# Values as the stationary operand in the dilated and the memory attention of a two-layer encoder

## The chip, the cores and the metric

The kernel runs on one core of a Trainium2 chip. The metric is the device time of one execution in microseconds (us). Engines are named as the profile names them: PE is TensorE's matmuls and PEld its weight loads, DVE is VectorE, ACT is ScalarE, POOL is GpSimd, SP is SyncE, whose queue issues the DMAs.

## What is computed

Two sequences of 256 tokens (512 rows in all) of width 1024 go through two layers. Layer 0 mixes with differential attention, layer 1 with dilated attention; each layer also attends with 4 heads of width 64 to 256 memory tokens, and ends with a gated ConvFFN. The parts that the change touches are the last steps of the two attentions:

```python
def memory_attention(xq, mk, mv):                 # both layers, 4 heads of 64
    s = einsum('bqhd,bkhd->bhqk', xq, mk) / sqrt(64)
    pr = softmax(s, axis=-1)
    return einsum('bhqk,bkhd->bqhd', pr, mv)

def dilated_mixer(...):                           # layer 1, 8 heads of 64, 3 groups of keys
    # per group: banded scores over residue classes, lse, pr = exp(s - lse), o = pr @ v
    w = softmax(stack(lses), axis=0)              # over the groups
    o = einsum('gbsh,gbshd->bshd', w, stack(outs))
```

The three groups of the dilated mixer, weighted by the softmax of their log-sums, are one softmax over all their keys together, and the kernel computes it so: for a tile of 128 queries and one head, the scores against 256 keys of group 0, 128 of group 1 and 128 of group 2 stand side by side in one 128x512 tile, with a mask.

## The kernel before

All activations of 512 tokens are four token tiles (NT = 4) of 128 rows; tiles 0 and 1 are one sequence, 2 and 3 the other. The large products (input projections, output projections, the ConvFFN) are split into a high and a low part: `mm3` (L368 to L370) issues three matmuls (high by high, low by high or high by low) for each 128 rows of contraction. Weights come by DMA (`w_loader`, L334), are split by ACT (L345) and DVE (L347), and wait in six pairs of buffers `wh` and `wl`.

The order of the work is made by a small planner that runs while the kernel is written (`Sched`): each part of the kernel is a generator that yields events or times; every `S.op(engine, cost)` advances that engine by a cost written beside the instruction, and the generator that is due next writes its instructions next. Each engine then runs its instructions in the order in which they were written, and waits where data are missing. So a changed cost or wait in one generator moves the instructions of all others around it. On PE the attention's small matmuls stand between `mm3` groups of the projections of the next pair of heads, or of the output projection at the end of the mixer.

The attention works on pairs of heads. For a token tile `t`, `scores` (L819) writes one 128x512 tile `sc` for each head of the pair; the heads lie on partitions 0 to 63 and 64 to 127 of the queries and keys, and their matmuls alternate. Then, for each head by itself (`unit`): DVE takes the minimum (L800 for memory, L1000 with the mask for dilated), ACT the exponential with its sum (L807, L1006), DVE the reciprocal of the sum into `rs` (L842, L1008), `transpose_e` (L742) turns the four 128x128 blocks of `e` on PE into a bank `tp` and ACT copies them to `eT` (L746), and four fp32 matmuls (L851 for memory, L1019 for dilated) with a block of `eT` as the stationary operand and 64 columns of the values moving add up 64 columns of the bank `o`, queries on partitions. An fp32 matmul shows as two records, one for each pass.

When all units are done, DVE multiplies the bank `o` by `rs` into `on` (L861, L1042), `out_T` (L774) transposes `on` on PE to features on partitions (with the permutation `perm_bwd` in layer 1), and `evac_seq` (L762 on ACT, L764 on DVE) splits the result into the high and low tiles that `out_proj` reads. Buffers: three `e`, three `eT`, two banks each of `sc` and `tp`, one bank `o`. The memory attention (`attn_cross`) runs once in each layer with 8 tiles-by-pairs, the dilated attention (`attn_b`) for four pairs of heads with 4 token tiles each. The differential attention (`attn_a`, L922) keeps its way through `transpose_e` and `out_T`.

Of the kernel before, what the change touches and what calls it, by code (L numbers as in the profile page):

```python
# [149 lines left out]
def c_dve(n, ptr=0, fast=False):  # L150
    return 0.15 + n / 960 + 0.06 * ptr
# [6 lines left out]
def c_mm(n, fp32=False):  # L158
    return n / 2400 * (4 if fp32 else 1) + 0.0135
# [99 lines left out]
def trunk_kernel(ctx: ExitStack, tc: tile.TileContext, io: dict, out: bass.AP):  # L259
# [31 lines left out]
    def sm(n, name):  # L291
        return small.tile([128, n], F32, tag=f"{name}{n}", name=name)
# [296 lines left out]
    def half(h):  # L589
        return slice(64 * h, 64 * h + 64)  # L590
# [177 lines left out]
    def out_T(o, cols, tiles, s, permuted):  # L768

        tp = yield from tp_s.get()  # L770
        for j in range(len(tiles)):
            for i in range(2):
                c = cols[j][i]
                nc.tensor.transpose(tp.v[:, (2 * j + i) * 128:(2 * j + i) * 128 + 128], o.v[:, c:c + 128],  # L774
                                    perm_bwd if permuted else ident)
                te = S.op("PE", T_PE)
        yield te
        for j, (hi, lo) in enumerate(tiles):
            yield from evac_seq(tp.v[:, 256 * j:256 * j + 256], hi, lo, s, permuted)
        tp.done(S.now)  # L780
# [4 lines left out]
        return hi, lo  # L785

    sc_lock = Lock(S)

    def sc_pair():
        yield from sc_lock.get()  # L790
# [37 lines left out]
    def attn_cross(xq_ev, mk_ev, mv_ev, permuted, res):  # L828
        yield xq_ev
        yield mk_ev  # L830
        yield mv_ev
        xqT, mkT, mv = xq_ev.val, mk_ev.val, mv_ev.val
        tiles = []
        for b in range(2):
            x = yield from hi_lo()
            tiles.append(x)
        parts = []

        def unit(t, h, sc, te, o_ev, rs, fin):
# [5 lines left out]
            yield o_ev  # L845
            o = o_ev.val.v.rearrange("p (t b h d) -> p t b h d", t=2, b=2, h=2)
            for b in range(2):
                for kt in range(2):
                    c = kt * 256 + (2 * b + h) * 64
                    i = 2 * b + kt  # L850
                    nc.tensor.matmul(o[:, t % 2, b, h, :], eT.v[:, i * 128:i * 128 + 128], mv[t // 2].v[:, c:c + 64],  # L851
                                     start=(kt == 0), stop=(kt == 1))
                    te = S.op("PE", c_mm(128, True))
            eT.done(te)
            fin.set(te)

        def finish(s, o_ev, rs, fins, part):
            for f in fins:
                yield f
            on = yield from on_s.get()  # L860
            nc.vector.tensor_tensor(on.v.rearrange("p (a d) -> p a d", d=64),  # L861
                                    o_ev.val.v.rearrange("p (a d) -> p a d", d=64),
                                    rs.rearrange("p t b h -> p (t b h)").unsqueeze(2).to_broadcast([128, 8, 64]),
                                    ALU.mult)
            te = S.op("DVE", c_dve(512))
            o_ev.val.done(te)
            yield te
            yield from out_T(on, [[0, 256], [128, 384]], tiles, s, permuted)
            on.done(S.now)
            part.set(S.now)  # L870

        for s in range(2):
            o_ev = S.event()
            rs = sm(8, "rs").rearrange("p (t b h) -> p t b h", t=2, b=2)
            fins = []
            for t in (2 * s, 2 * s + 1):
                sc = yield from sc_pair()
                te = scores(sc, [(256 * b, xqT[b], slice(t * 128, t * 128 + 128), mkT[b],
                                  slice(s * 256, s * 256 + 256)) for b in range(2)])
                for h in range(2):  # L880
                    f = S.event()
                    fins.append(f)
                    S.spawn(unit(t, h, sc[h], te, o_ev, rs, f))
                if t % 2 == 0:
                    S.spawn(take(o_s, o_ev))
            part = S.event()
            parts.append(part)
            S.spawn(finish(s, o_ev, rs, fins, part))
# [98 lines left out]
    def attn_b(q01, q2k0, k12, v01_ev, v2_ev, vcol, last_v2, res):  # L987
        for x in (q01, q2k0, k12):
            yield x
        q = [q01.val[0], q01.val[1], q2k0.val[0]]  # L990
        k = [q2k0.val[1], k12.val[0], k12.val[1]]
        o_ev = S.event()
        rs = sm(8, "rs").rearrange("p (t h) -> p t h", h=2)

        def unit(t, h, sc, te, fin):
            s, qi = divmod(t, 2)
            yield te
            e = yield from e_s.get()
            mn = sm(1, "mn")
            nc.vector.tensor_tensor_reduce(out=e.v, in0=sc.v, in1=mask[:, qi, :], scale=1.0, scalar=BIG,  # L1000
                                           op0=ALU.add, op1=ALU.min, accum_out=mn)
# [9 lines left out]
            yield o_ev  # L1011
            yield v01_ev
            yield v2_ev
            v = [(v01_ev.val, 0), (v01_ev.val, 128), (v2_ev.val, vcol)]
            o = o_ev.val.v.rearrange("p (t h d) -> p t h d", t=NT, h=2)
            for i, (g, kt) in enumerate(((0, 0), (0, 1), (1, qi), (2, qi))):
                vt, c = v[g]
                c += kt * 256 + 64 * h
                nc.tensor.matmul(o[:, t, h, :], eT.v[:, i * 128:i * 128 + 128], vt[s].v[:, c:c + 64],  # L1019
                                 start=(i == 0), stop=(i == 3))  # L1020
                te = S.op("PE", c_mm(128, True))
            eT.done(te)
            fin.set(te)

        fins = []
        for t in range(NT):
            tq = slice(t * 128, t * 128 + 128)
            ks = slice(t // 2 * 256, t // 2 * 256 + 256)
            sc = yield from sc_pair()
            te = scores(sc, [(0, q[0], tq, k[0], ks), (256, q[1], tq, k[1], tq), (384, q[2], tq, k[2], tq)])  # L1030
            for h in range(2):
                f = S.event()
                fins.append(f)
                S.spawn(unit(t, h, sc[h], te, f))
            if t == 0:
                S.spawn(take(o_s, o_ev))
        for f in fins:
            yield f
        for x in q + k + v01_ev.val + (v2_ev.val if last_v2 else []):
            x.done(S.now)  # L1040
        on = yield from on_s.get()
        nc.vector.tensor_tensor(on.v.rearrange("p (a d) -> p a d", d=64),  # L1042
                                o_ev.val.v.rearrange("p (a d) -> p a d", d=64),
                                rs.rearrange("p t h -> p (t h)").unsqueeze(2).to_broadcast([128, 8, 64]),
                                ALU.mult)
        te = S.op("DVE", c_dve(512))
        o_ev.val.done(te)
        yield te
        tile_ = yield from hi_lo()
        for s in range(2):  # L1050
            yield from out_T(on, [[256 * s, 256 * s + 128]], [tile_], s, True)
        on.done(S.now)
        res.set(S.now, tile_)


# [479 lines left out]
```

## Time and profile before

| what | value |
|---|---|
| median of 3 runs | 1406.17 us (1405.69 to 1406.70) |
| the profiled execution's own time | 1404.72 us |
| its span | 1402.9 us |
| PE busy | 1385.6 us, 99% of the span |
| DVE / ACT / POOL busy | 55% / 44% / 20% |

The span runs from the first to the last instruction of the profiled execution. Busy time counts each moment at which at least one instruction of the engine runs. A PE row's duration holds the time until its last result is written, so the rows of neighbouring matmuls overlap; what a matmul takes of PE's time is read from the start of one row to the start of the next. A row of the timeline may merge several instructions of one line (x8, x16); then its start is that of the first.

### The profile page before, as it was taken

Reading aid. Unit: us, or ns where it says so; the run is one execution under the profiler, and the core shown is the slowest. Engines: PE = TensorE matmul, PEld = TensorE weight load, DVE = VectorE, ACT = ScalarE, POOL = GpSimd, SP = SyncE. Lnnn points to the kernel's source line nnn. Section 1 sums busy time; section 2 is a strip of 40 time slices with the busy share of each in tenths; the row PEclk is TensorE's granted clock in tenths of the full one; section 3 lists DMA queues with packets and bytes.
Section 4 is the critical chain, followed back from the end, with each engine's and each line's share of the span. In section 5 each row is a group of like instructions: output and inputs, shape, how many; then the busy total and the mean of one; then the engine's idle time right before and its main releaser. Section 6 shows DMA issues by size and latency. Waiting matters only on the chain.

```text
span 1402.9 us, 18598 instructions
## 1 busy us (share of the span) xinstructions
PE 1385.6 (99%) x7072; PEld 1155.9 (82%) x7072; DVE 772.9 (55%) x1244; ACT 610.7 (44%) x1107; POOL 284.3 (20%) x608
## 2 busy tenths in 40 slices
PE   7899999999999999999999999999999999999998
PEld 5678788889888888888888888888898888888887
DVE  5665657886664365535754344443567562466353
ACT  6566455544342244324445534443545441334131
POOL 3727653120000000010064074535010000000000
PEclk9999999999999999999999999999999999999999
DMA  8531212233333333424321211232123323333321
GB/s 285 186 114 52 73 63 61 68 99 106 105 90 98 97 96 100 152 67 142 81 84 61 61 61 61 71 105 66 57 79 109 102 90 106 90 105 91 98 68 61
DMA packets 42106, 131.97 MB, mean 94 GB/s; under 512 B 6048, under 2 KB 6944, under 8 KB 42016
## 3 DMA queue, kind: packets, MB, share of 16 engines
q1 hardware_dynamic: 42016, 130.77, 30.5%
q8 instruction: 56, 0.92, 0.3%
q14 instruction: 34, 0.28, 0.1%
HBM read 128.65 MB, written 2.10 MB: 93 GB/s over the span
## 4 chain that ended last, share of the span: by engine, by line
PE 98%; DMA 1%; ACT 0%; DVE 0%; SPq 0%; issue 0%; ACTq 0%; DVEq 0%
PE acc L368 20%; PE acc L369 20%; PE acc L370 20%; PE sc L368 7%; PE sc L369 7%; PE sc L370 7%; PE sc L819 3%; PE tp L742 2%; PE o L1019 2%; PE tp L647 2%; PE o L370 1%; PE o L369 1%; PE o L368 1%; PE o L922 1%; PE o L851 1%; PE tp L488 1%
## 5 line engine op out<-in xcount | busy, mean ns | idle before, releaser
L347 DVE TENSOR_TENSOR wl<-raw,wh 128x1024 fp32r<-128x1024 f32 (+1 forms) x222 | 270.1, 1219 | 280.0 <-ACT wh L345 279.2
L345 ACT CAST wh<-raw 128x1024 fp32r<-128x1024 f32 (+1 forms) x222 | 231.8, 1046 | 387.1 <-PE sc L369 187.5
L368 PE MATMUL acc<-wh,hh 128*128 128x512 f32 (+1 forms) x536 | 217.7, 406 | 13.3 <-ACT wh L345 6.7
L369 PE MATMUL acc<-wl,hh 128*128 128x512 f32 (+1 forms) x536 | 204.4, 381 | 0.1
L370 PE MATMUL acc<-wh,hl 128*128 128x512 f32 (+1 forms) x536 | 204.3, 381 | 0.0
L368 PE MATMUL acc<-wh,blk 128*128 128x512 f32 x368 | 148.4, 403 | 0.0
L370 PE MATMUL acc<-wh,blk 128*128 128x512 f32 x368 | 143.6, 390 | 0.0
L369 PE MATMUL acc<-wl,blk 128*128 128x512 f32 x368 | 143.5, 390 | 0.0
L368 PE MATMUL acc<-hh,wh 128*128 128x512 f32 (+1 forms) x384 | 143.1, 373 | 0.0
L368 PE MATMUL sc<-hh,wh 128*128 128x512 f32 (+1 forms) x384 | 142.9, 372 | 0.0
L369 PE MATMUL acc<-hl,wh 128*128 128x512 f32 (+1 forms) x384 | 142.6, 371 | 0.0
L370 PE MATMUL acc<-hh,wl 128*128 128x512 f32 (+1 forms) x384 | 142.6, 371 | 0.0
L369 PE MATMUL sc<-hl,wh 128*128 128x512 f32 (+1 forms) x384 | 142.6, 371 | 0.0
L370 PE MATMUL sc<-hh,wl 128*128 128x512 f32 (+1 forms) x384 | 142.6, 371 | 0.0
L368 PEld LDWEIGHTS acc<-wh,hh 128*128 128x128 f32 x536 | 102.0, 190 | 34.3 <-ACT sq L605 7.8
L614 POOL TENSOR_SCALAR ss<-ss,nrms 128x4 f32<-128x4 f32 x96 | 32.6, 339 | 480.3 <-DVE ss L608 476.0
L370 PEld LDWEIGHTS acc<-wh,hl 128*128 128x128 f32 x536 | 101.9, 190 | 20.0
L369 PEld LDWEIGHTS acc<-wl,hh 128*128 128x128 f32 x536 | 102.4, 191 | 14.6 <-DVE wl L347 0.6
L615 POOL TENSOR_TENSOR rstd<-ss,mhalf 128x4 f32<-128x4 f32 x96 | 102.6, 1069 | 8.0
L368 PEld LDWEIGHTS sc<-hh,wh 128*128 128x128 f32 x384 | 72.3, 188 | 12.5
L369 PEld LDWEIGHTS sc<-hl,wh 128*128 128x128 f32 x384 | 72.3, 188 | 12.5
L370 PEld LDWEIGHTS acc<-hh,wl 128*128 128x128 f32 x384 | 72.3, 188 | 12.5
(151 smaller groups left out, 2251.6 us busy)
## 6 DMA issues: line engine op xcount, KB each, us to landing
raw<-w SPq DMA_DIRECT2D x218, 512.0 KB, 3.6
blk<-xT SPq DMA_DIRECT2D x8, 256.0 KB, 6.7
X<-x SPq DMA_DIRECT2D x4, 512.0 KB, 4.4
blk<-memT SPq DMA_DIRECT2D x8, 256.0 KB
blk<-mem SPq DMA_DIRECT2D x8, 256.0 KB
qn<-memT SPq DMA_DIRECT2D x8, 256.0 KB, 5.3
y<-X SPq DMA_DIRECT2D x8, 256.0 KB, 2.0
raw<-w SPq DMA_DIRECT2D x4, 256.0 KB, 3.3
```

The lines of the kernel that those rows point to most:

```text
L345: nc.scalar.copy(hi.v[:, a], r.v[:, a])
L347: nc.vector.tensor_tensor(lo.v[:, a], r.v[:, a], hi.v[:, a].bitcast(F32), ALU.subtract)
L368: nc.tensor.matmul(out_, ah, bh, start=start, stop=False)
L369: nc.tensor.matmul(out_, ah, bl, start=False, stop=False)
L370: nc.tensor.matmul(out_, al, bh, start=False, stop=stop)
L488: nc.tensor.transpose(tp.v[:, k * 128:k * 128 + 128], h[j].v[:, k * 128:k * 128 + 128], perm_fwd if permuted else ident)
L614: nc.gpsimd.tensor_scalar(ss, ss, 1.0 / 64, nr[key, t][0], ALU.mult, ALU.add)
L615: nc.gpsimd.tensor_tensor(rstd, ss, mhalf[:, 0:4], ALU.pow)
L647: nc.tensor.transpose(tp.v[:, x * 128:x * 128 + 128], src[:, x % 2, b * 128:b * 128 + 128], ident)
L742: nc.tensor.transpose(tp.v[:, i * 128:i * 128 + 128], e.v[:, i * 128:i * 128 + 128], ident)
L819: nc.tensor.matmul(sc[h].v[:, c:c + n], q.v[half(h), tq], k.v[half(h), ks], start=True, stop=True)
L1019: nc.tensor.matmul(o[:, t, h, :], eT.v[:, i * 128:i * 128 + 128], vt[s].v[:, c:c + 64], start=(i == 0), stop=(i == 3))
```

## The change

In the memory and the dilated attention the roles of the two operands are swapped. The 64 columns of a head's values become the stationary operand (128x64), and a 128x128 block of `eT` moves. The result is the output transposed: 64 features of a head on partitions, 128 queries along the bank. The head of index 0 in a pair writes partitions 0 to 63 of `o`, that of index 1 partitions 64 to 127, and their matmuls alternate (`values_by_heads`). Since the sums then no longer lie on partitions of the output, each `e` is multiplied by the reciprocal of its sum before it is transposed (a DVE instruction of 128x512 in each unit). `out_T` is not called there any more: in layer 1 `perm_bwd` stands in place of the identity in the transposition of `e`, and `evac_seq` reads the bank `o` itself. Both heads' transposed tiles are taken under one lock, one after the other, before the pair's value matmuls; a unit hands its `e` over by an event.

```diff
-    def transpose_e(e, n):
+    def transpose_e(e, n, perm=None):
...
-            nc.tensor.transpose(tp.v[:, i * 128:i * 128 + 128], e.v[:, i * 128:i * 128 + 128], ident)
+            nc.tensor.transpose(tp.v[:, i * 128:i * 128 + 128], e.v[:, i * 128:i * 128 + 128],
+                                perm if perm is not None else ident)
...
+    eT_lock = Lock(S)
+
+    def values_by_heads(o, parts, es, n, perm, evs, fin):
+        for ev in evs:
+            yield ev
+        for ev in es:
+            yield ev
+        yield from eT_lock.get()
+        eT = []
+        for ev in es:
+            x = yield from transpose_e(ev.val, n, perm)
+            eT.append(x)
+        eT_lock.put()
+        for i, cols, vs, first, last in parts():
+            for h in range(2):
+                nc.tensor.matmul(o.val.v[half(h), cols], vs[h], eT[h].v[:, i * 128:i * 128 + 128], start=first,
+                                 stop=last)
+            S.op("PE", c_mm(128, True))
+        te = S.op("PE", 0.35)
...
 # attn_cross: unit
-            nc.vector.reciprocal(rs[:, t % 2, :, h], ssum)
-            S.op("DVE", 0.16)
-            eT = yield from transpose_e(e, 4)
...
-                    nc.tensor.matmul(o[:, t % 2, b, h, :], eT.v[:, i * 128:i * 128 + 128], mv[t // 2].v[:, c:c + 64],
-                                     start=(kt == 0), stop=(kt == 1))
+            rs = sm(2, "r")
+            nc.vector.reciprocal(rs, ssum)
+            ev = e.v.rearrange("p (b k) -> p b k", b=2)
+            nc.vector.tensor_tensor(ev, ev, rs.unsqueeze(2).to_broadcast([128, 2, 256]), ALU.mult)
...
 # attn_cross: finish
-            nc.vector.tensor_tensor(on.v.rearrange("p (a d) -> p a d", d=64),
-                                    o_ev.val.v.rearrange("p (a d) -> p a d", d=64),
...
-            yield from out_T(on, [[0, 256], [128, 384]], tiles, s, permuted)
+            for b in range(2):
+                yield from evac_seq(o_ev.val.v[:, 256 * b:256 * b + 256], *tiles[b], s, permuted)
...
 # attn_b: unit
-            nc.vector.reciprocal(rs[:, t, h:h + 1], ssum)
-            S.op("DVE", 0.16)
-            eT = yield from transpose_e(e, 4)
...
-                nc.tensor.matmul(o[:, t, h, :], eT.v[:, i * 128:i * 128 + 128], vt[s].v[:, c:c + 64],
-                                 start=(i == 0), stop=(i == 3))
+            rs = sm(1, "c1")
+            nc.vector.reciprocal(rs, ssum)
+            nc.vector.tensor_scalar(e.v, e.v, rs, None, ALU.mult)
...
 # attn_b: end
-        for s in range(2):
-            yield from out_T(on, [[256 * s, 256 * s + 128]], [tile_], s, True)
+        for s in range(2):
+            for f in fins[2 * s:2 * s + 2]:
+                yield f
+            yield from evac_seq(o_ev.val.v[:, 256 * s:256 * s + 256], *tile_, s, True)
```

The planner writes a new order around this. PE, in the dilated attention's last pair of heads, one token tile before the change (`tp<-ident,e` is a transposition, `o<-` a value matmul, `acc<-` the output projection):

```order
L742 MATMUL tp_9443<-ident,e_9385 128x128 x4
L1019 MATMUL o_9316<-blk_9171,eT_9390 128x64 x3
L1019 MATMUL o_9316<-blk_8560,eT_9390 128x64
L742 MATMUL tp_9453<-ident,e_9418 128x128 x4
L368 MATMUL acc_9458<-wh_9092,blk_7478 128x512
L369 MATMUL acc_9458<-wl_9093,blk_7478 128x512
L370 MATMUL acc_9458<-wh_9092,blk_7479 128x512
L1019 MATMUL o_9316<-blk_9171,eT_9442 128x64 x3
L1019 MATMUL o_9316<-blk_8560,eT_9442 128x64
```

And now, the same pair of heads, from the first head's transposition of that tile's successor to its value matmuls:

```order
L742 MATMUL tp_9520<-perm_bwd,e_9449 128x128 x4
...
L742 MATMUL tp_9563<-perm_bwd,e_9472 128x128 x4
...
L370 MATMUL acc_9586<-wh_9140,blk_6706 128x512
L806 MATMUL o_9318<-eT_9519,blk_9284 64x128
L806 MATMUL o_9318<-eT_9562,blk_9284 64x128
...
L806 MATMUL o_9318<-eT_9519,blk_8710 64x128
L806 MATMUL o_9318<-eT_9562,blk_8710 64x128
L368 MATMUL acc_9586<-wh_9140,blk_6707 128x512
```

The two heads' groups of four have become one group of eight whose neighbours belong to different heads; three and four `mm3` of the output projection stand between the two transpositions and behind the second.

PE, the last token tile of the last pair before the change:

```order
L742 MATMUL tp_9512<-ident,e_9481 128x128 x4
L368 MATMUL acc_9502<-wh_9077,blk_8260 128x512
L369 MATMUL acc_9502<-wl_9078,blk_8260 128x512
L370 MATMUL acc_9502<-wh_9077,blk_8261 128x512
L1019 MATMUL o_9316<-blk_9250,eT_9494 128x64 x3
L1019 MATMUL o_9316<-blk_8744,eT_9494 128x64
L368 MATMUL acc_9526<-wh_9092,blk_7478 128x512
L369 MATMUL acc_9526<-wl_9093,blk_7478 128x512
L370 MATMUL acc_9526<-wh_9092,blk_7479 128x512
L1019 MATMUL o_9316<-blk_9250,eT_9511 128x64 x3
L1019 MATMUL o_9316<-blk_8744,eT_9511 128x64
```

And PE at the last token tile of the last pair now (`tp<-perm_bwd,e` is a transposition of a head's `e`):

```order
L370 MATMUL acc_9586<-wh_9140,blk_6708 128x512
L742 MATMUL tp_9605<-perm_bwd,e_9516 128x128 x4
L742 MATMUL tp_9613<-perm_bwd,e_9543 128x128 x4
L806 MATMUL o_9318<-eT_9604,blk_9284 64x128
L806 MATMUL o_9318<-eT_9612,blk_9284 64x128
...
L806 MATMUL o_9318<-eT_9604,blk_8710 64x128
L806 MATMUL o_9318<-eT_9612,blk_8710 64x128
L368 MATMUL acc_9629<-wh_9307,blk_8892 128x512
```

Here nothing stands any more between the last transpositions and the value matmuls that read their copies; before, an `mm3` and the other head's work stood there.

## Rows read from the trace of the kernel before

**Rows 1.** The page: busy times, granted clock (tenths of full speed), chain by engine.

```profile
PE 1385.6 (99%) x7072; PEld 1155.9 (82%) x7072; DVE 772.9 (55%) x1244; ACT 610.7 (44%) x1107; POOL 284.3 (20%) x608
PEclk9999999999999999999999999999999999999999
PE 98%; DMA 1%; ACT 0%; DVE 0%; SPq 0%; issue 0%; ACTq 0%; DVEq 0%
```

**Rows 2.** Busy time by stretches: nearly all, memory attentions of both layers, dilated attention.

```profile
core 0: us, PE busy (x) PEld busy (x) DVE busy (x) ACT busy (x) POOL busy (x), PEclk, DMA share, GB/s
60.00:1400.00 1340.00, 1338.93 (x6890) 1119.01 (x6887) 738.81 (x1173) 575.23 (x1041) 256.61 (x542) 1.00 0.29 87
109.00:132.00 23.00, 23.00 (x144) 18.65 (x143) 13.55 (x32) 15.13 (x48) 13.87 (x33) 1.00 0.00 1
738.00:762.00 24.00, 24.00 (x161) 20.32 (x161) 11.60 (x25) 14.13 (x39) 11.07 (x24) 1.00 0.08 25
776.00:1018.00 242.00, 242.00 (x1448) 205.15 (x1446) 105.05 (x223) 111.12 (x212) 94.86 (x216) 1.00 0.22 70
```

**Rows 3.** Timeline of PE and PEld, 994 to 999 us: start, duration, instructions.

```profile
994.63 0.40 PE L370 MATMUL acc<-wh,blk 128*128 128x512 f32 x1
994.96 0.96 PEld L819 LDWEIGHTS sc<-blk,blk 64*128 64x128 f32 x12 [0.37 <-DVE rs L1008]
994.96 1.15 PE L819 MATMUL sc<-blk,blk 64*128 64x256 f32 x12
996.04 0.51 PE L368 MATMUL acc<-wh,blk 128*128 128x512 f32 x1
996.38 0.40 PE L369 MATMUL acc<-wl,blk 128*128 128x512 f32 x1
...
997.17 1.87 PEld L1019 LDWEIGHTS o<-blk,eT 128*128 128x128 f32 x16
997.28 1.90 PE L1019 MATMUL o<-blk,eT 128*128 128x64 f32 x16
```

**Rows 4.** Timeline, 1004 to 1014 us: transposition, copy, value matmuls, `mm3`, `out_T`.

```profile
1004.25 0.61 PE L742 MATMUL tp<-ident,e 128*128 128x128 f32 x4
1004.95 0.59 ACT L746 COPY eT<-tp 128x512 f32<-128x512 f32 x1 [0.42 <-PE tp L742]
...
1010.71 0.40 PE L370 MATMUL acc<-wh,blk 128*128 128x512 f32 x1
1010.94 1.00 PE L1019 MATMUL o<-blk,eT 128*128 128x64 f32 x8
1011.75 0.47 PE L368 MATMUL acc<-wh,blk 128*128 128x512 f32 x1
1012.06 0.39 PE L369 MATMUL acc<-wl,blk 128*128 128x512 f32 x1
...
1012.99 0.39 PE L370 MATMUL acc<-wh,blk 128*128 128x512 f32 x1
1013.22 0.38 PE L774 MATMUL tp<-perm_bwd,on 128*128 128x128 f32 x2
...
1013.67 0.40 PE L369 MATMUL acc<-wl,blk 128*128 128x512 f32 x1
```

**Rows 5.** All value matmuls by line: durations in ns, first and last start.

```profile
L1019 PE MATMUL o<-blk,eT x256: 217/275/275, 794.4 to 1011.7; 128*128 128x64 f32 x128
L851 PE MATMUL o<-blk,eT x128: 217/275/275, 116.0 to 760.1; 128*128 128x64 f32 x128
```

**Rows 6.** Timeline of PE in the differential attention: 128 columns moving, 128 stationary.

```profile
227.41 1.50 PE L922 MATMUL o<-blk,eT 128*128 128x128 f32 x12
228.66 0.48 PE L368 MATMUL acc<-wh,blk 128*128 128x512 f32 x1
```

**Rows 7.** DVE instructions near the added ones: count, minimum, median and maximum in ns.

```profile
L911 DVE TENSOR_SCALAR e<-e,c x32: 352/353/450, 78.7 to 268.2; 128x256 f32<-128x256 f32 x32
L1042 DVE TENSOR_TENSOR on<-o,rs x4: 691/692/692, 807.9 to 1012.0; 128x512 f32<-128x512 f32 x4
```

More of the change, by code (lines that the diff above doesn't have):

```diff
@@ L787, in trunk_kernel @@
     sc_lock = Lock(S)
+    eT_lock = Lock(S)
[16 more added lines that the diff above has]
+        te = S.op("PE", 0.35)
+        for x in eT:
+            x.done(te)
+        fin.set(te)
     def sc_pair():
@@ L837, in attn_cross, with unit @@
         parts = []
[L839 removed]
+        def unit(sc, te, ready):
             yield te
             e, ssum = yield from softmax2(sc)
[L842 to L855 removed]
@@ L857, in finish, with parts_of, parts @@
-        def finish(s, o_ev, rs, fins, part):
+            rs = sm(2, "r")
+            nc.vector.reciprocal(rs, ssum)
+            ev = e.v.rearrange("p (b k) -> p b k", b=2)
+            nc.vector.tensor_tensor(ev, ev, rs.unsqueeze(2).to_broadcast([128, 2, 256]), ALU.mult)
+            yield S.op("DVE", 0.16 + c_dve(512))
+            ready.set(S.now, e)
+        def parts_of(t):
+            def parts():
+                for b in range(2):
+                    for kt in range(2):
+                        c = kt * 256 + 2 * b * 64
+                        yield (2 * b + kt, slice(256 * b + t % 2 * 128, 256 * b + t % 2 * 128 + 128),
+                               [mv[t // 2].v[:, c:c + 64], mv[t // 2].v[:, c + 64:c + 128]], kt == 0, kt == 1)
+            return parts
@@ L858, in finish @@
+        def finish(s, o_ev, fins, part):
             for f in fins:
                 yield f
-            on = yield from on_s.get()
-            nc.vector.tensor_tensor(on.v.rearrange("p (a d) -> p a d", d=64),
-                                    o_ev.val.v.rearrange("p (a d) -> p a d", d=64),
-                                    rs.rearrange("p t b h -> p (t b h)").unsqueeze(2).to_broadcast([128, 8, 64]),
-                                    ALU.mult)
-            te = S.op("DVE", c_dve(512))
@@ L866, in finish @@
-            o_ev.val.done(te)
-            yield te
-            yield from out_T(on, [[0, 256], [128, 384]], tiles, s, permuted)
-            on.done(S.now)
+            for b in range(2):
+                yield from evac_seq(o_ev.val.v[:, 256 * b:256 * b + 256], *tiles[b], s, permuted)
+            o_ev.val.done(S.now)
             part.set(S.now)
@@ L879, in attn_cross @@
                                   slice(s * 256, s * 256 + 256)) for b in range(2)])
[L880 to L883, printed above, removed]
                 if t % 2 == 0:
                     S.spawn(take(o_s, o_ev))
+                f = S.event()
+                fins.append(f)
+                es = [S.event(), S.event()]
+                for h in range(2):
+                    S.spawn(unit(sc[h], te, es[h]))
+                S.spawn(values_by_heads(o_ev, parts_of(t), es, 4, perm_bwd if permuted else None, [o_ev], f))
             part = S.event()
             parts.append(part)
-            S.spawn(finish(s, o_ev, rs, fins, part))
+            S.spawn(finish(s, o_ev, fins, part))
         for part in parts:
@@ L992, in attn_b, with unit @@
         o_ev = S.event()
-        rs = sm(8, "rs").rearrange("p (t h) -> p t h", h=2)
-        def unit(t, h, sc, te, fin):
-            s, qi = divmod(t, 2)
+        def unit(t, sc, te, ready):
             yield te
@@ L999, in unit @@
             mn = sm(1, "mn")
-            nc.vector.tensor_tensor_reduce(out=e.v, in0=sc.v, in1=mask[:, qi, :], scale=1.0, scalar=BIG,
+            nc.vector.tensor_tensor_reduce(out=e.v, in0=sc.v, in1=mask[:, t % 2, :], scale=1.0, scalar=BIG,
                                            op0=ALU.add, op1=ALU.min, accum_out=mn)
@@ L1007, in unit, with parts_of, parts @@
             yield S.op("ACT", c_act(512, 1, 1))
-            nc.vector.reciprocal(rs[:, t, h:h + 1], ssum)
-            S.op("DVE", 0.16)
-            eT = yield from transpose_e(e, 4)
[L1011 to L1018, printed above, removed]
-                nc.tensor.matmul(o[:, t, h, :], eT.v[:, i * 128:i * 128 + 128], vt[s].v[:, c:c + 64],
-                                 start=(i == 0), stop=(i == 3))
-                te = S.op("PE", c_mm(128, True))
-            eT.done(te)
-            fin.set(te)
+            rs = sm(1, "c1")
+            nc.vector.reciprocal(rs, ssum)
+            nc.vector.tensor_scalar(e.v, e.v, rs, None, ALU.mult)
+            yield S.op("DVE", 0.16 + c_dve(512))
+            ready.set(S.now, e)
+        def parts_of(t):
+            s, qi = divmod(t, 2)
+            def parts():
+                v = [(v01_ev.val, 0), (v01_ev.val, 128), (v2_ev.val, vcol)]
+                for i, (g, kt) in enumerate(((0, 0), (0, 1), (1, qi), (2, qi))):
+                    vt, c = v[g]
+                    c += kt * 256
+                    yield (i, slice(t * 128, t * 128 + 128), [vt[s].v[:, c:c + 64], vt[s].v[:, c + 64:c + 128]],
+                           i == 0, i == 3)
+            return parts
         fins = []
@@ L1030, in attn_b @@
             te = scores(sc, [(0, q[0], tq, k[0], ks), (256, q[1], tq, k[1], tq), (384, q[2], tq, k[2], tq)])
[L1031 to L1034, printed above, removed]
             if t == 0:
                 S.spawn(take(o_s, o_ev))
-        for f in fins:
-            yield f
+            f = S.event()
+            fins.append(f)
+            es = [S.event(), S.event()]
+            for h in range(2):
+                S.spawn(unit(t, sc[h], te, es[h]))
+            S.spawn(values_by_heads(o_ev, parts_of(t), es, 4, perm_bwd, [o_ev, v01_ev, v2_ev], f))
+        tile_ = yield from hi_lo()
+        for s in range(2):
+            for f in fins[2 * s:2 * s + 2]:
+                yield f
+            yield from evac_seq(o_ev.val.v[:, 256 * s:256 * s + 256], *tile_, s, True)
+        o_ev.val.done(S.now)
         for x in q + k + v01_ev.val + (v2_ev.val if last_v2 else []):
             x.done(S.now)
[L1041 to L1049, printed above, removed]
-        for s in range(2):
-            yield from out_T(on, [[256 * s, 256 * s + 128]], [tile_], s, True)
-        on.done(S.now)
         res.set(S.now, tile_)
```

1 line of the change is left out of this document (removed).

## The prediction, made before the changed kernel was run

> **What bounds the kernel now.** I read the page first. PE is busy for 99% of the span, PE makes up 98% of the chain that ended last, and its clock is granted in full in every slice [rows 1]. The table by stretches says the same of the places that change: over the dilated attention (242 us) and in both memory attentions (23 and 24 us) PE is busy for the whole of each stretch, while DVE has 43 to 59% and ACT 46 to 66% [rows 2]. From 60 to 1400 us PE lacks 1.07 us of 1340 [rows 2]. So this kernel is a row of PE instructions without holes, and the attention's small matmuls, though they stand among projections, are all on the path: what they give up comes off the time, and what another engine does is free until PE waits for it.
>
> **What a value matmul costs now.** A plain 512-column matmul takes 0.23 us from start to start (L370 at 1010.71, the next at 1010.94) [rows 4]. One head of one token tile, eight records, stands between that L370 and the L369 at 1012.06: 1.35 us, less two plain steps, 0.89 us, or 0.11 us a record [rows 4]. There are 256 + 128 records [rows 5], so 48 such groups: 48 x 0.89 = 42.7 us. Only 64 columns move in each, yet twelve records of the differential attention, with 128 columns moving against a stationary block of the same size, take 1.25 us or 0.104 us each [rows 6]. So half the moving columns bought nothing: each record waits for its 128 stationary columns.
>
> **What goes with out_T.** Two transpositions of `on` between the L370 at 1012.99 and the L369 at 1013.67: 0.68 less 0.46, 0.22 us, 0.11 us each [rows 4]. The memory attentions have 8 in each layer, the dilated one 4 in each of four pairs: 32, or 3.5 us. The transpositions of `e` stay as many as they were; `perm_bwd` costs what the identity costs. Together 42.7 + 3.5 = 46.2 us of PE's time go.
>
> **What comes.** 24 groups of eight matmuls (16 records), each pair of neighbours on the two halves of the stationary columns. The trace of before has no matmul that uses half of the columns, so the price must come from the nearest row, the scores, which pair the two heads on the two halves of the rows. A dilated score group has 12 records: two heads, two passes, 256 + 128 + 128 columns, so 1024 columns for each head. It takes 994.63 to 996.38, 1.75 less 0.46, 1.29 us [rows 3]. At the 0.104 us that one record needs for 128 columns [rows 6], 2048 columns one after the other would be 1.66 us without any cost of changing over; 1024 would be 0.83 us. So the two heads do run side by side there, and about 0.46 us go to the way in and out. The new group also has 1024 columns for each head (eight records of 128). By this row it costs 1.29 us. I take off a little: its loads are half as long, so the first, which nothing covers, saves about 0.05 us, and eight of the 24 groups are followed at once by transpositions, which share the way back. I take 1.25 us, between 1.20 and 1.30: 24 x 1.25 = 30.0 us. The bounds for the unknown are wider: without any changing over 24 x 0.83 = 20 us; with the two halves one after the other 16 x 0.104 + 0.46 = 2.12 us, 24 of them 51 us. I take the value near the score row, since it is the same engine with the same pass pairs and the same kind of pairing.
>
> **What the other engines get.** DVE gains one instruction over 128x512 in each of 48 units, about 0.69 us each as the multiplication at L1042 (256 columns took 0.35 us at L911) [rows 7], and loses eight at L1042 and L861: about 27 us more. In the dilated attention that is 32 x 0.69 - 4 x 0.69 = 19 us on 105 of 242 [rows 2]. It is hidden as long as PE finds other work; the new order puts at least one `mm3` and mostly more between a head's transposition and the value matmuls. ACT and SP have the same instructions as before, two copies of `eT` in a row included. Behind the new DVE multiplication wait, in DVE's queue, the next head's mask and the splits of weights; six buffers of split weights lie ahead of PE.
>
> **One new wait I do see.** At the last tile of the last pair eight transpositions are followed at once by the value matmuls. A copy starts 0.70 us after the first of its four transpositions and takes 0.59 [rows 4]. Two sets back to back occupy PE for 0.88 us; the first copy ends at 1.29, the second at 1.88, and PE waits about 1.05 us; I write 1.1. The split of the output behind it is hidden: its first half is done earlier, and the products that need the second half stand behind eight others. If the second head's multiplication is late there (two weight splits stand ahead of it on DVE), the wait grows by one or two us.
>
> **The sum.** -46.2 + 30.0 + 1.1 = -15.1 us. The profiled execution takes 1404.72 us, 1.4 below the median of the runs; the sum applied to the median of 1406.17 gives **1391.1 us** (a span near 1387.8).
>
> **A rule against it.** Rows 3 show the 16 weight loads of a value group running from 997.17 to 999.04, underneath their matmuls (997.28 to 999.18), all on the same 128 rows: a load does lie beside the matmul before it. The Trainium skill, "TensorE: Matmul & The Clock Gate", part 3, says that weight loads overlap with matmuls in flight only when their row groups differ, and part 2 adds the background weight buffer as a second case; two halves of the columns share all row groups. By the rows the loads cost nothing; by the first sentence they would be laid bare, and the change would lose.
>
> **Rivals.**
> Loads laid bare (slower). If a load for one half can't run while the other half streams, each group pays for 16 loads of 64 columns. Sixteen of 128 take 1.87 us [rows 3], so these cost about 0.9 us, 24 groups 22 us: -15.1 + 22 = +7, 1413 us. The change turns into a loss once more than two thirds of that show. For it: the halves of the columns share the rows, which the score pairs don't. Against it: loads are under the matmuls in every group now. That case is the form in which the quoted rule would come true. 6%.
>
> The halves don't run side by side. Then the group costs 2.12 us at most, 51 us in all, and the sum is -46.2 + 51 + 1.1 = +6, 1412 us; without the cost of changing over 40 us, -5 us, 1401. For it: no row shows two streams of 128 rows each entering at once; in the scores each stream has 64 rows. Against it: nothing but the pattern of the scores. 7%, of which 4% slower, 2% within 0.2%.
>
> PE now waits for the chain. The chain of a tile is longer by 0.69 us, heads wait for one another under the lock, and three `eT` serve two at a time. If each of the 24 groups waited 0.3 us more, 7 us would go: 1398; at 0.6 us all but nothing is left, 1405. For it: PE has to take its order as written. Against it: the new order has other work between nearly all steps, and today PE loses 1 us in 1340. 10% for a loss of 4 to 10 us, 3% for more.
>
> **How the numbers follow.** The forecast (1391, with 1387 to 1395 as its own range: 1.10 to 1.40 us a group, the wait 0 to 2 us) has 74%. The range for 8 in 10 takes in the forecast and the milder half of the waiting case: 1386 to 1399. A measurement of this kernel can tell about 0.2%, 2.8 us, from no change. Faster by more than that (below 1403.4): 74 + 10 + 1 + 1 = 86%; within: 4%; slower: 10%.
>
> **What would show it.** In the profile after, sixteen value records between a plain L370 and the following L369 should take about 1.25 us beyond the two plain steps, their starts in pairs a few ns apart, and 24 such groups must be there; 2.1 us shows that the halves run one after the other, or with loads bare. PE's records should be 32 fewer, PE still 99% busy, DVE busy near 800 us. A hole of about 1 us in PE ahead of the last value group is due, and no others. I am wrong if PE shows waits for ACT's copy or DVE's multiplication ahead of many groups, or if the groups cost over 1.5 us.

## The result and the profile after

| | before | after |
|---|---|---|
| median of 4 runs | 1405.93 us | 1391.27 us (1389.82 to 1392.80) |
| the profiled execution's own time | | 1389.82 us |
| its span | | 1388.0 us |

The ratio is 0.9898, 95% interval 0.9886 to 0.9910: 1.0% faster. 1391.1 us was forecast.

The page of the changed kernel; the first line is busy time, the second the granted clock, the third the chain that ended last by engine:

```profile
PE 1368.7 (99%) x7040; PEld 1127.5 (81%) x7040; DVE 793.8 (57%) x1284; ACT 611.8 (44%) x1107; POOL 293.0 (21%) x608
PEclk9999999999999999999999999999999999999999
PE 94%; POOL 3%; DVE 1%; DMA 1%; ACT 1%; issue 1%; SPq 0%; ACTq 0%; POOLq 0%; DVEq 0%
```

Against [rows 1]: PE has 32 records fewer, as counted, and is still busy for 99%. DVE has 20.9 us more. New is POOL with 3% of the chain, where it had no share before. That is how long the chain now runs through POOL's queue, and not what is lost by it; the waits below have the price.

The value matmuls now, and the same 0.23 us steps around them; the timeline of PE and of ACT at two places, a group in the middle of the last pair of heads and that pair's last group:

```profile
985.15 0.40 PE L370 MATMUL acc<-wh,blk 128*128 128x512 f32 x1
985.48 1.09 PE L806 MATMUL o<-eT,blk 128*64 128x128 f32 x16
986.50 0.50 PE L368 MATMUL acc<-wh,blk 128*128 128x512 f32 x1
986.84 0.39 PE L369 MATMUL acc<-wl,blk 128*128 128x512 f32 x1
...
1000.80 0.39 PE L370 MATMUL acc<-wh,blk 128*128 128x512 f32 x1
1001.02 1.03 PE L742 MATMUL tp<-perm_bwd,e 128*128 128x128 f32 x8
1002.30 1.58 PE L806 MATMUL o<-eT,blk 128*64 128x128 f32 x16 [0.24 <-ACT eT L747]
1003.81 0.50 PE L368 MATMUL acc<-wh,blk 128*128 128x512 f32 x1
1004.15 0.40 PE L369 MATMUL acc<-wl,blk 128*128 128x512 f32 x1
...
1001.66 1.08 ACT L747 COPY eT<-tp 128x512 f32<-128x512 f32 x2 [4.23 <-PE tp L742]
```

A group: 985.15 to 986.84 is 1.69 us, less two plain steps 1.23 us, where two groups of eight took 2 x 0.89 [rows 4]. It resembles the score group of [rows 3] (1.29 us) at both ends: 0.33 us instead of 0.23 from the L370 before it, 0.34 from L368 to L369 behind it. Added up in this way, the 24 groups take 29.9 us: 1.23 us in the 14 that an `mm3` follows, 1.18 in the 9 that a transposition follows, and 2.02 for the last one. That one waits for the copies, as the PE rows say: its 16 records take 1.51 us to the next L368 instead of 1.02, and start 0.3 us later than eight transpositions alone would let them. So 0.8 us of the 29.9 are waiting and 29.1 the groups.

Where PE waited for another engine, in total, times and the longest, over the whole span of the changed kernel:

```profile
PE acc L368 <- ACT wh L345: 7.0, 1, 7.0
PE acc L368 <- DVE qn L619: 3.8, 2, 2.1
PE tp L647 <- POOL qn L634: 2.7, 3, 1.4
PE acc L368 <- ACT sq L605: 1.8, 1, 1.8
PE o L806 <- ACT eT L747: 0.2, 1, 0.2
```

Three of these lines stood there before (6.7, 4.8 and 1.8 us); they lie in the first 55 us. Two are new. The line on POOL was not foreseen: PE reaches the transposition of queries and keys before POOL has rotated them, at 69 us (1.0 us), at 141 us (1.4 us) and at 967 us (0.3 us). These are idle times, counted from the end of the row before, and a row lasts longer than its step. Read from start to start, as all other prices here, PE loses 1.15, 1.57 and 0.46 us there beyond the plain step of 0.11 us between transpositions.

### The profile page after: what moved, and what is told of

It reads as the page before. It is cut to its first block, busy times and chain, and to the rows that moved or that the text cites. A ratio compares the mean times of both kernels' runs of the same rounds, so it can differ in the third digit from the quotient of the medians.

```text
span 1388.0 us, 18552 instructions
## 1 busy us (share of the span) xinstructions
PE 1368.7 (99%) x7040; PEld 1127.5 (81%) x7040; DVE 793.8 (57%) x1284; ACT 611.8 (44%) x1107; POOL 293.0 (21%) x608
## 4 chain that ended last, share of the span: by engine, by line
PE 94%; POOL 3%; DVE 1%; DMA 1%; ACT 1%; issue 1%; SPq 0%; ACTq 0%; POOLq 0%; DVEq 0%
PE acc L368 20%; PE acc L369 19%; PE acc L370 19%; PE sc L368 8%; PE sc L370 8%; PE sc L369 8%; PE sc L844 3%; PE tp L742 2%; PE o L806 2%; PE tp L647 1%; PE o L369 1%; PE o L370 1%; PE o L368 1%; PE o L943 1%; POOL rstd L615 1%; PE tp L488 1%
## 5 line engine op out<-in xcount | busy, mean ns | idle before, releaser
L368 PE MATMUL acc<-wh,hh 128*128 128x512 f32 (+1 forms) x536 | 217.4, 406 | 12.7 <-ACT wh L345 7.0
L369 PE MATMUL acc<-wl,hh 128*128 128x512 f32 (+1 forms) x536 | 204.0, 381 | 0.1
L370 PE MATMUL acc<-wh,hl 128*128 128x512 f32 (+1 forms) x536 | 203.9, 380 | 0.0
L368 PE MATMUL acc<-wh,blk 128*128 128x512 f32 x368 | 148.4, 403 | 0.0
L370 PE MATMUL acc<-wh,blk 128*128 128x512 f32 x368 | 143.6, 390 | 0.0
L369 PE MATMUL acc<-wl,blk 128*128 128x512 f32 x368 | 143.6, 390 | 0.0
L368 PE MATMUL acc<-hh,wh 128*128 128x512 f32 (+1 forms) x384 | 143.1, 373 | 0.0
L368 PE MATMUL sc<-hh,wh 128*128 128x512 f32 (+1 forms) x384 | 142.9, 372 | 0.0
L369 PE MATMUL acc<-hl,wh 128*128 128x512 f32 (+1 forms) x384 | 142.6, 371 | 0.0
L370 PE MATMUL sc<-hh,wl 128*128 128x512 f32 (+1 forms) x384 | 142.6, 371 | 0.0
L370 PE MATMUL acc<-hh,wl 128*128 128x512 f32 (+1 forms) x384 | 142.6, 371 | 0.0
L369 PE MATMUL sc<-hl,wh 128*128 128x512 f32 (+1 forms) x384 | 142.6, 371 | 0.0
L368 PEld LDWEIGHTS acc<-wh,hh 128*128 128x128 f32 x536 | 101.8, 190 | 36.5 <-issue 7.0
L370 PEld LDWEIGHTS acc<-wh,hl 128*128 128x128 f32 x536 | 101.6, 190 | 20.0
L369 PEld LDWEIGHTS acc<-wl,hh 128*128 128x128 f32 x536 | 102.1, 191 | 14.6 <-DVE wl L347 0.6
L615 POOL TENSOR_TENSOR rstd<-ss,mhalf 128x4 f32<-128x4 f32 x96 | 106.8, 1113 | 8.0
L370 PEld LDWEIGHTS sc<-hh,wl 128*128 128x128 f32 x384 | 72.3, 188 | 12.5
L370 PEld LDWEIGHTS acc<-hh,wl 128*128 128x128 f32 x384 | 72.3, 188 | 12.5
L369 PEld LDWEIGHTS sc<-hl,wh 128*128 128x128 f32 x384 | 72.3, 188 | 12.5
```

What stands on the lines that cost most here:

```text
L368: nc.tensor.matmul(out_, ah, bh, start=start, stop=False)
L369: nc.tensor.matmul(out_, ah, bl, start=False, stop=False)
L370: nc.tensor.matmul(out_, al, bh, start=False, stop=stop)
L615: nc.gpsimd.tensor_tensor(rstd, ss, mhalf[:, 0:4], ALU.pow)
```

## The experiments

The theory was that the whole gain is PE's time in the value groups, because the two heads run side by side on the two halves of the stationary columns, with the transpositions that `out_T` no longer makes. The rivals were loads laid bare, halves in turn, a chain that PE waits for, and a gain that comes from the new order. The changed kernel was also run again beside the first experiments, as their measure.

### The changed kernel again

> The changed kernel once more, as the measure for the others. Theory (the two heads' value matmuls run side by side on the two halves of the stationary columns): 1391 us, groups of 16 records at 1.21 us each. PE in the first profile waited three times for POOL ahead of the transpositions of queries and keys (983, 1405 and 297 ns). If these belong to the order of the changed kernel they stand here again at the same places; if they are chance they don't.

Measured: 1392.39 us, ratio 0.9905 (0.9889 to 0.9920). The waits for POOL stand at the same three places of the program, 0.95, 1.39 and 0.28 us, so they are not chance alone. Which of them come from the change, the next runs told.

The two medians of this one program lie 1.1 us apart, and its first score matmul starts at 74.4 us in the first profile and at 77.1 us in the second. So the experiments below also give the time of the two attentions alone, from each kernel's profile: from the first score matmul to the first transposition of the ConvFFN's input in layer 0, and from the last transposition of layer 1's input to the first of its ConvFFN's input, added up. Before, that is 544.5 us; in both profiles of the changed kernel it is 531.0 us, the two within 0.02 us.

### A whole head after the other

```diff
-        for i, cols, vs, first, last in parts():
-            for h in range(2):
+        for h in range(2):
+            for i, cols, vs, first, last in parts():
...
```

> One edit: the four value matmuls of the first head are issued before the four of the second, where they alternated. All else stays, the order of the rest too. Theory: side by side is the whole gain, and matmuls start in program order, so the groups fall apart into 16 records one after the other: 16 x 0.104 + 0.4 = 2.1 us against 1.21, 24 x 0.86 = 21 us more: 1412 us, slower than before. Rival (the gain comes from the 32 dropped transpositions, the shorter end and the shorter loads, not from running side by side): 1391 to 1394 us. Rival (matmuls of the other half are pulled ahead whatever the order): groups stay at 1.21 us, 1391 us.

Measured: 1402.17 us, ratio 0.9973 (0.9964 to 0.9982), 10 us more than the changed kernel; the two attentions take 541.0 us, 10.0 us more. Every engine has the same instructions in the same order as there, but for these matmuls. It is neither the 21 us of the theory nor the nothing of the rivals. The timeline of PE at a group of this kernel:

```profile
995.78 0.40 PE L370 MATMUL acc<-wh,blk 128*128 128x512 f32 x1
996.10 1.58 PE L806 MATMUL o<-eT,blk 128*64 128x128 f32 x16
997.61 0.50 PE L368 MATMUL acc<-wh,blk 128*128 128x512 f32 x1
997.95 0.39 PE L369 MATMUL acc<-wl,blk 128*128 128x512 f32 x1
```

2.17 us less 0.46 is 1.71 us, 0.48 us more than with alternation. Added up over all 24 groups it is 11.2 us, since the last group takes 2.02 us in either order. About 1 us came back, since PE waited 0.4 instead of 1.4 us for POOL at 144 us. Inside the group the steps from start to start, in ns, read from the trace for this group and, above it, for the group of the changed kernel shown before; the last number is the step to the L368:

```
heads alternate      7 153 7 102 7 102 7 103 6 103 6 103 7 102 7 202
a whole head first 160 110 109 109 6 103 57 52 57 52 57 109 109 110 109 202
```

The trace doesn't name the head of a record; it follows from the steps, since records of one half are over 0.1 us apart, and from the load that carries the wait for the second head's copy. With alternation all starts come in pairs, 7 ns apart, a pair every 0.109 us. With a whole head first, four records run alone at 0.109 us; then the second head's first record (its load has that wait) starts 6 ns behind the first head's fifth, while three records of the first head still wait. From there eight records start every 0.055 us in the mean, two streams at once; then the second head's last four are alone. So running side by side is what makes the gain, and PE looks ahead past a few waiting records, which the theory had not reckoned with.

### Two and two

```diff
-        for i, cols, vs, first, last in parts():
+        ps = list(parts())
+        for two in (ps[0:2], ps[2:4]):
             for h in range(2):
...
+                for i, cols, vs, first, last in two:
...
```

> The order between the changed kernel (heads alternate) and the one with a whole head after the other: two matmuls (four records) of the first head, two of the second, two of the first, two of the second. With a whole head first, the second head's first record started together with the first head's fifth, past three records that still waited. Theory (PE starts a record on a free half past at most three that wait): four records of the other head are just not too many, both halves are always busy, groups stay at 1.21 us, 1392 us. Rival (the look-ahead is shorter, or counts loads as well): each turn leaves one half idle for a step or more, 0.1 to 0.3 us a group, 1394.5 to 1399 us.

Measured: 1392.64 us, ratio 0.9900 (0.9882 to 0.9918), as the changed kernel; the two attentions take 531.9 us, 1.0 us more. PE's timeline at a group, and the steps of its records:

```profile
987.91 0.40 PE L370 MATMUL acc<-wh,blk 128*128 128x512 f32 x1
988.24 1.15 PE L808 MATMUL o<-eT,blk 128*64 128x128 f32 x16
989.31 0.50 PE L368 MATMUL acc<-wh,blk 128*128 128x512 f32 x1
989.65 0.39 PE L369 MATMUL acc<-wl,blk 128*128 128x512 f32 x1
```

```
two and two         13 147 13 96 14 95 14 96 13 96 56 53 57 52 57 202
```

Both halves are busy from the first record to the last; at the end one half lags by half a step, 0.05 us a group (1.28 against 1.23). Four records of one head in a row are not too many, eight are. The starts of both kernels agree with a look-ahead past three waiting records; the exact rule was not sought further.

### 64 moving columns, twice the loads

```diff
-        for i, cols, vs, first, last in parts():
...
+        for m in (0, 64):
+            for i, cols, vs, first, last in parts():
+                c = slice(cols.start + m, cols.start + m + 64)
+                for h in range(2):
+                    nc.tensor.matmul(o.val.v[half(h), c], vs[h], eT[h].v[:, i * 128 + m:i * 128 + m + 64], ...
```

> Each value matmul of the changed kernel is cut into two of 64 moving columns, each with its own load of the 64 stationary columns: 32 records a group instead of 16, the same columns in all. Theory (in the changed kernel the 128 moving columns set the step of a pair, 0.109 us; loads of the two halves run beside each other and beside the streams): a pair's step falls to some 0.055 us, a group stays at 1.2 to 1.3 us, 1392 us. Rival (loads of the two halves queue on one path, at 0.055 each, and only just fit under 128 columns; the rule that loads overlap only between row groups): the step of a pair stays at 0.11 us, a group takes 16 x 0.11 + 0.4 = 2.1 us, 24 x 0.87 = 21 us more, 1413 us.

Measured: 1393.34 us, ratio 0.9915 (0.9899 to 0.9931); the two attentions take 532.0 us, 1.1 us more than in the changed kernel. The timeline of PE at a group:

```profile
988.67 0.40 PE L370 MATMUL acc<-wh,blk 128*128 128x512 f32 x1
989.00 1.15 PE L808 MATMUL o<-eT,blk 128*64 128x64 f32 x32
990.08 0.50 PE L368 MATMUL acc<-wh,blk 128*128 128x512 f32 x1
990.42 0.39 PE L369 MATMUL acc<-wl,blk 128*128 128x512 f32 x1
```

32 records with 32 loads take 1.75 less 0.46, 1.29 us: 0.06 us more than 16 records with 16 loads of the same columns. A pair starts every 0.058 us. In that time two loads of 64 columns and two streams of 64 columns lie beside each other, all on the same 128 rows. The loads take 0.14 us each in the trace and start in pairs too, 7 ns apart. So loads of the two halves do not take turns, and the rival of bare loads, which needed 0.11 us for a pair, is refuted. The sentence of the Trainium skill ("TensorE: Matmul & The Clock Gate", part 3) that loads overlap with matmuls in flight only when the row groups differ does not hold for halves of the columns here.

### Twice as many visits

```diff
-        for i, cols, vs, first, last in parts():
+        for j, (i, cols, vs, first, last) in enumerate(parts()):
...
             S.op("PE", c_mm(128, True))
+            if j == 1:
+                yield S.op("PE", 0.35, 0)
```

> Each group of eight value matmuls is written as two of four, with whatever is due on PE between them. Theory (a group of the changed kernel costs 0.87 us of streams and 0.31 to 0.36 us for changing over, whatever its length): 24 further visits, 7.5 to 8.6 us more, 1400 us. Rival (the overhead goes with the matmuls, not with the visits): 1392 us.

Measured: 1396.78 us, ratio 0.9938 (0.9923 to 0.9954), 4.4 to 5.5 us more than the changed kernel where 8 were expected; the two attentions take 536.5 us, 5.5 us more. The timeline of PE at a half group, and where PE waited from 60 us on:

```profile
1005.19 0.40 PE L370 MATMUL acc<-wh,blk 128*128 128x512 f32 x1
1005.52 0.66 PE L806 MATMUL o<-eT,blk 128*64 128x128 f32 x8
1006.10 0.50 PE L368 MATMUL acc<-wh,blk 128*128 128x512 f32 x1
1006.44 0.40 PE L369 MATMUL acc<-wl,blk 128*128 128x512 f32 x1
```

```profile
PE tp L647 <- POOL qn L634: 1.2, 2, 0.9
```

1.25 less 0.46 is 0.79 us for eight records, 1.23 for sixteen: 0.44 us go with eight records, and 0.35 us with the visit. The price of a visit is as expected, the total is not. All 48 half groups take 37.5 us, 7.6 more than the 24 with their 0.8 us of waiting. The rest is in the waits: in this order PE doesn't wait at the last tile (counted in the 7.6 already), and not for POOL at 141 us either, 1.6 us from start to start. 7.6 less 1.6 is 6.0, where the two attentions show 5.5; the last 0.5 us were not placed.

### DVE's new work doubled

```diff
             nc.vector.tensor_scalar(e.v, e.v, rs, None, ALU.mult)
+            nc.vector.tensor_scalar(e.v, e.v, 1.0, None, ALU.mult)
```

The same line stands behind the multiplication in the memory attention.

> Behind the multiplication of each numerator a second one by 1.0 on DVE (128x512, 48 times, about 0.49 us each, 23 us in all); the planner isn't told, so every engine keeps its order. Theory (DVE's work ahead of the transpositions is hidden behind projections, except at the last tile): 0.5 to 1.5 us more, 1392 to 1393.5 us, one longer wait at the last tile. Rival (the longer chain of a tile is what PE now waits for): most of the 24 groups wait 0.5 to 1 us more, 1404 us and above.

Measured: 1391.18 us, ratio 0.9902 (0.9880 to 0.9923). The two added groups on DVE (busy us and mean ns), PE at the last group, and where PE waited for POOL:

```profile
L1031 DVE TENSOR_SCALAR e<-e 128x512 f32<-128x512 f32 x32 | 13.7, 428 | 1.1
L871 DVE TENSOR_SCALAR e<-e 128x512 f32<-128x512 f32 x16 | 6.8, 428 | 0.5
...
1001.65 1.03 PE L742 MATMUL tp<-perm_bwd,e 128*128 128x128 f32 x8
1002.92 1.58 PE L806 MATMUL o<-eT,blk 128*64 128x128 f32 x16 [0.24 <-ACT eT L747]
1004.43 0.50 PE L368 MATMUL acc<-wh,blk 128*128 128x512 f32 x1
```

```profile
PE tp L647 <- POOL qn L634: 1.9, 2, 1.7
```

20.5 us more on DVE cost 0.3 us: the two attentions take 531.2 us, and the one wait that grew is that for POOL at 141 us, 1.66 instead of 1.40 us. No value group pays. At the last tile PE takes 1.27 and 1.51 us, 1.28 and 1.51 in the changed kernel. So the chain through DVE has more slack than its added length ahead of the groups, and no part of the wait at the last tile is DVE's; it is the two copies on ACT.

### Each attention alone

The changed kernel with the memory attention of before, and with the dilated attention of before (whole functions exchanged).

> The change in the dilated attention alone, the memory attention as before. Theory: of 48 groups of eight records 32 go (32 x 0.89 = 28.5 us) with 16 transpositions (1.8 us), 16 groups of 1.21 us come (19.4 us) and 0.8 us of waiting at the last tile: 10.1 us less than before, 1396 us. Rival (the gain comes from the new order around the groups): the two parts don't add up to the whole.

> The change in the memory attention of both layers alone, the dilated attention as before. Theory: 16 groups at 0.89 us (14.2 us) and 16 transpositions (1.8 us) go, 8 groups at 1.21 us (9.7 us) come: 6.3 us less than before, 1399.6 us. With the dilated part alone that makes 16.4 us against the 14.7 us measured for both; the difference would be the waits for POOL. Rival (order): the parts don't add up to the whole.

Measured: 1396.36 us (ratio 0.9934, 0.9917 to 0.9951) and 1400.62 us (0.9960, 0.9945 to 0.9975), so 9.5 and 5.2 us less than before. They add up to 14.7 us; both together gave 14.7 in the first comparison and 13.4 in this one. In the two attentions it is 8.7 and 4.9 us, together 13.6, and 13.6 for both at once: the parts add up to the whole. Where PE waited for others from 60 us on, dilated alone and then memory alone:

```profile
PE tp L647 <- POOL qn L634: 1.3, 2, 0.9
PE o L806 <- ACT eT L747: 0.2, 1, 0.2
```

```profile
PE tp L647 <- POOL qn L634: 2.3, 2, 1.4
```

The 1.4 us at 141 us are there with the memory attention alone and not with the dilated one; the 0.3 us near 970 us the other way round. The 0.9 us at 71 us stand in both, though up to 110 us every engine has the same instructions in the same order as before the change. This wait is missing in the profiles of before, of the doubled DVE work and of the late tables. So the waits at 141 and 967 us are owed to the change and the one near 70 us is not: it comes and goes with the start, which differed by up to 2.7 us between these profiles (the first score matmul started at 74.4 us in the first profile of the changed kernel, at 77.1 in the second, at 75.4 before).

### POOL's tables later

From 132 to 143 us POOL works through 24 small products that make the rotation tables of layer 1; their first reader starts at 707 us. The timeline of POOL ahead of the wait in the changed kernel, and PE's rows there, the last of which waits:

```profile
138.10 0.22 POOL L1344 TENSOR_TENSOR rope_b<-blk 128x16 f32<-128x16 f32 x1
...
139.37 0.23 POOL L1347 TENSOR_TENSOR rope_b<-blk 128x16 f32<-128x16 f32 x1
139.70 0.27 POOL L614 TENSOR_SCALAR ss<-ss,nrms 128x4 f32<-128x4 f32 x1
140.05 1.01 POOL L615 TENSOR_TENSOR rstd<-ss,mhalf 128x4 f32<-128x4 f32 x1
...
141.84 0.72 POOL L634 TENSOR_TENSOR qn<-ropew 128x64 f32<-128x64 f32 x1
```

```profile
140.72 0.49 PE L647 MATMUL tp<-ident,qn 128*128 128x128 f32 x3
142.61 0.33 PE L647 MATMUL tp<-ident,qn 128*128 128x128 f32 x1 [1.41 <-POOL qn L634]
```

```diff
+        yield 300.0
         yield from table(st, ("b0", 1, (1, 2)), ("b1", 1, (3, 5)), ("b2", 1, (6, 7)))
```

> The changed kernel with one edit: POOL writes the rotation tables of layer 1 300 us later by the planner's clock, behind the attention of layer 0, where they now stand ahead of the rotation of queries at 141 us. Theory (the wait of PE for POOL at 141 us, 1.4 us, comes from the tables in POOL's queue, which the faster PE no longer covers): the wait is gone and the time is 1.4 us lower, near 1390 us, the best of all kernels. Rival (the wait comes from the planner's own reckoning of the rotation): the wait stays, 1391.5 us.

Measured: 1389.11 us, ratio 0.9891 (0.9870 to 0.9912), the lowest median of all kernels. PE's waits from 60 us on, and the same rotation on POOL and transposition on PE:

```profile
PE tp L647 <- POOL qn L634: 0.3, 1, 0.3
PE o L806 <- ACT eT L747: 0.2, 1, 0.2
```

```profile
139.43 0.33 POOL L634 TENSOR_TENSOR qn<-ropew 128x64 f32<-128x64 f32 x1
140.62 0.60 PE L647 MATMUL tp<-ident,qn 128*128 128x128 f32 x4
```

The wait is gone: POOL has rotated the queries at 139.76 us, and PE asks for them at 140.62. In the changed kernel POOL had them at 142.56, and eight of the products, from 138.10 to 139.60 us, stood in its queue ahead of the steps that PE waited for. The planner's order on PE changed as well, from 140 us on, so the products are not the only difference; PE asks one `mm3` sooner in its order, though, which would lengthen a wait. Layer 0's attention takes 222.4 us instead of 224.1 and layer 1's the same 306.8: 1.7 us less, about what the wait cost from start to start. The medians alone would not show it: this one lies 2.2 and 3.3 us below the two of the changed kernel, which lie 1.1 us apart themselves, its own runs reach from 1388.86 to 1393.57 us, and the intervals overlap.

## Why the prediction held, step by step

- **What bounds the kernel.** Right: PE stayed at 99%, and PE's own time is what moved. From the first score matmul to the first transposition of the ConvFFN's input, layer 0 takes 225.8 us before and 224.1 after. From the last transposition of layer 1's input to the first of its ConvFFN's input it is 318.7 and 306.8 us. The ConvFFNs between and behind take the same (385.4 and 385.5, 373.0 and 373.0 us). So 13.6 us went in the two attentions. Of the 14.9 us between the spans of the two profiles another 1.0 lies ahead of the first score matmul, in the start, which varies by up to 2.7 us from profile to profile, and 0.4 behind PE's last matmul.
- **What goes, 46.2 us.** Right. Added up over all rows of the trace before, the value matmuls took 42.6 us against 42.7; 32 transpositions are gone.
- **What comes, 30.0 us.** Right in kind and nearly in size: 29.1 us. The score group was the right stand-in, and the deductions were the right ones: 1.23 us before an `mm3` and 1.18 before a transposition, where 1.25 was taken for all (and nine groups, not eight, are followed by transpositions). The visit's overhead is a price of its own (0.35 us), as doubling the visits showed.
- **DVE's work hidden.** Right, with more room than claimed: twice the work was hidden as well, but for 0.3 us at POOL. Its size was taken too high in the dilated attention: 0.49 us for an instruction, where 0.69 was written.
- **The wait at the last tile, 1.1 us.** Right in place and cause, 0.8 us in size: the first head's first two records started (0.16 us apart in the trace) while the second head's copy still ran. The prediction's own terms give 1.00 us (1.88 - 0.88), where 1.05 was read.
- **No other holes.** Wrong. POOL was in no term of the sum. The prediction looked for waits in the chain of the attention itself; it did not ask which other queue the faster and reordered PE would meet. 1.57 and 0.46 us were owed to this, from start to start. They more than offset the cheaper groups and the cheaper last wait (0.9 + 0.3 us): -46.2 + 29.1 + 0.8 + 2.0 = -14.3 us, where -15.1 was forecast. The medians say 14.7 us in the first comparison and 13.4 in the second, the stages of the two profiles 13.6; the 0.7 us between this sum and the stages were not placed. That the forecast lies 0.2 us from the first median is luck within this; the same program's second median is 1.3 us above it.
- **The rivals.** Bare loads are refuted by the kernel with twice the loads, halves in turn by the trace and by the kernel with a whole head first; a chain that PE waits for by the doubled DVE work. A gain from the new order alone is refuted by the kernel with a whole head first too: it keeps the order around the groups and loses 10.0 of the 13.6 us. The expectation for a whole head first failed in size, since it took matmuls to start strictly in the order written.

## What to carry to other kernels

Where PE is the bound and matmuls have 64 useful columns, look at what sets the step of a record: here 64 moving columns waited for 128 stationary ones, and swapping the operands put two heads on the array at once. Price such a pairing by a group that already pairs in the same trace, overhead of the visit included, and make visits few and long. Then ask which queue the faster engine will run into next, on engines that the edit never mentions.

## What the runs showed of the hardware

- Two fp32 matmuls on the two halves of the stationary columns ran side by side, 128 rows moving in both: 0.109 us for a pair of records with 128 moving columns, as long as for one record alone (in the kernel with a whole head first), and 0.058 us for a pair with 64, loads included.
- Going from full-width matmuls to a group on halves of the columns and back cost 0.31 us (a transposition follows, 1.18 - 8 x 0.109) to 0.36 us (an `mm3` follows, 1.23 - 8 x 0.109), and as much for groups of half the length (0.79 - 4 x 0.109).
- Matmuls did not start strictly in the order written: a record for a free half started 6 ns behind the fifth of the other half, while three earlier ones still waited. So that each engine runs its instructions in the order in which they were written does not hold for PE's halves here. The Trainium skill ("TensorE: Matmul & The Clock Gate", part 3) says that matmuls keep program order in start and end; for starts on different halves the step list of the kernel with a whole head first speaks against it.
